# Moving the adaLN steps and the norm's scale and bias in a two-layer decoder trunk

## The chip, the cores and the metric

One core of a Trainium2 chip runs the whole program. The metric is device time in microseconds (us). A core has five engines that run side by side, each through its own instructions in order: TensorE (PE, matrix multiplication), VectorE (DVE), ScalarE (ACT), GpSimd (POOL) and SyncE (SP), which here issues all the DMAs that load data.

## What is computed

A trunk of two layers on 512 tokens of width 1024, all in float32. Each layer has three sub-layers: a SwiGLU feed-forward part (FFN), a token mixer (retention, dilated attention and stick-breaking attention on one input projection) and a second FFN. Each is modulated by a shift, a scale and a gate which come from the vector `c` (adaLN), and each ends in a norm:

```python
cond = jax.nn.silu(c)
for l in range(DEPTH):                                   # DEPTH = 2
    mod = cond @ w_ada[l] + b_ada[l]                     # (1024) x (1024, 9 * 1024)
    sh1, sc1, g1, sh2, sc2, g2, sh3, sc3, g3 = split(mod, 9)
    y = swiglu(x * (1 + sc1) + sh1, ffn1_w_gate[l], ffn1_w_up[l], ffn1_w_down[l])
    x = post_norm(x, y, g1, 0.5, ln_gain[l, 0], ln_bias[l, 0])
    y = token_mixer(x * (1 + sc2) + sh2, w_in[l], w_out[l])
    x = post_norm(x, y, g2, 1.0, ln_gain[l, 1], ln_bias[l, 1])
    y = swiglu(x * (1 + sc3) + sh3, ffn2_w_gate[l], ffn2_w_up[l], ffn2_w_down[l])
    x = post_norm(x, y, g3, 0.5, ln_gain[l, 2], ln_bias[l, 2])
# post_norm(x, y, gate, w, gain, bias) = layer_norm(ALPHA * x + w * (1 + gate) * y) * gain + bias
```

## The kernel before

**Tiles.** The residual `xall` is kept in the core as four tiles of 128 tokens by 1024 (`xres[t]`). The input of a sub-layer, `hT`, is its modulated transpose (128 by 8 by 512). All matrix products are made in three passes from a rounded high part and the remainder: `unit` (lines 168 to 178) loads 512 KB of weights into a buffer `raw`, ACT rounds it to `hi` (line 176) and VectorE subtracts to get `lo` (line 177). `raw` has three buffers, `hi` and `lo` four each. `mm3` (181 to 183) and `rows_mm` (375, 376, 379) are the three passes on TensorE.

**An FFN** (`ffn`) has 11 groups of gate and up columns, each of four units, every unit 24 matmuls; `glu` (391 to 394) makes the activation of a group. The first group's units are loaded ahead, by the sub-layer before, and its tokens are run in two halves of 256: the second half of `hT` is not there yet. Then 18 units of the down projection run over all tokens, and the last four (`RES`) token tile by token tile, with the norm of each tile behind it. The first FFN of layer 0 has three columns done in the startup.

**The norm** (`PostNorm`). `tile(t)` adds the product to the residual (312, 313), takes the statistics (315, 318), the inverse root on POOL (145, 146), the shift `nmr` (330), and normalises on ACT (331), without gain and bias: these are folded into the scale and shift columns of the next input. `head` makes the first half of the next input from tiles 0 and 1, and `rest`, called in the next sub-layer after three units of its first group, makes the second half, both through `make_h`: transposes on TensorE (275), scale and shift on ACT (279) and VectorE (281), rounding on ACT (285), remainder on VectorE (286). Each passes through `htmp`, which has three buffers. `rest` then puts gain and bias into the residual itself by eight POOL instructions of 128 by 1024 (lines 365 and 366, two for each tile), issued behind the last inverse root.

**The adaLN steps** (`ada`). A vector of 1024 values of `mod` takes eight steps (each loads 512 KB of `w_ada` into a `raw` buffer and adds it, times a column of `cond`, to an accumulator on VectorE, lines 198 to 202), a sum over partitions on POOL (206) and a small end on VectorE (215, 216 or 219). The steps stand in a list `bg`: 63 entries in the first FFN, 53, 43 and 13 in the three others; the mixers have none. `drain(3)` issues three of them after each group and `drain(2)` two after each down unit. On VectorE a step is ordered behind `mods["nmr"]`, the `nmr` of the last norm tile. Accumulators, sums, gates, and the rows of gain and bias share four buffers (`bcp`).

**Order.** The program's order is a priority; a scheduler lays out each engine's queue from it at compile time, and each queue then runs in order. `issue_after` is a constraint on that layout. So a DMA on SP that waits for a buffer holds the DMAs behind it.

**A mixer** works through ten projection jobs of two units each (`sk`, `dv`, `dq`, `dk`, `rv`, `rv2`, `rq`, `rk`, `rg`, `rg2`), whose matmuls fill TensorE between the steps of the three kinds of heads. `drain(1)` at the end of a job finds an empty list.

Of the kernel before, what the change touches and what calls it, by code (L numbers as in the profile page):

```python
# [13 lines left out]
ALU = mybir.AluOpType  # L14
# [4 lines left out]
T = 512  # L19
NT = T // P  # L20
KC = D // P
FF = 2816
NF = FF // P
# [44 lines left out]
def trunk(ctx: ExitStack, tc: tile.TileContext, x_in, c_in, w_ada, b_ada, ln_gain, ln_bias,  # L68
          f1g, f1u, f1d, w_in, w_out, f2g, f2u, f2d, rope_t, decay_t, logc_t, out, depth=DEPTH):
    nc = tc.nc  # L70
    V, S, G, PE = nc.vector, nc.scalar, nc.gpsimd, nc.tensor
# [78 lines left out]
    xres = [xall[:, t, :] for t in range(NT)]  # L150

    def gain_col(l, s):
        o = (l * 3 + s) * KC
        return cols[:, o:o + KC]
# [9 lines left out]
    mods = {}  # L164
# [79 lines left out]

    POST = 3
    bg = []

    def drain(n):
        for _ in range(min(n, len(bg))):
            bg.pop(0)()  # L250


    def new_h():
# [40 lines left out]

    class PostNorm:
        def __init__(self, l, s, nxt):
            self.l, self.s, self.nxt = l, s, nxt
            self.gate = mods[("g", l, s)]
            self.gain = bcast_row(ln_gain[l, s])
            self.bias = bcast_row(ln_bias[l, s])  # L300
            self.h = None
            if nxt is not None:
                self.h = new_h()
                self.a, self.b = ab(nxt[0], nxt[1], gain_col(l, s), bias_col(l, s))
# [55 lines left out]
        def rest(self):  # L360

            ends = make_h(1, self.h, self.a, self.b)
            with tc.issue_after(self.last.ins):
                for t in range(NT):
                    G.tensor_tensor(out=xres[t], in0=xres[t], in1=self.gain, op=ALU.mult)
                    G.tensor_tensor(out=xres[t], in0=xres[t], in1=self.bias, op=ALU.add)
            return ends


# [37 lines left out]
    REST_AT = 3  # L407
    REST_AT_Q = 3
    LAST_CUT = (256, 256, 512, 1024)
    DRAIN = (3, 2)  # L410
    RES = 4
    ACT_HEADS = (1, 3)
    OUT_EARLY = 2
# [5 lines left out]
    def ffn(l, s, wg, wu, wd, h, pre, gt, rest, prefetch, nxt):  # L419
        hh, hl = h  # L420
        ends = None
        groups = []
        f = len(gt)
        while f < NF:
            n = 2 if f + 2 <= NF else 1
            groups.append((f, n))
            f += n
        for gi, (f, n) in enumerate(groups):
            pss = [[psum() for _ in range(n)] for _ in range(2)]
            first = gi == 0 and pre is not None  # L430
            if gi == 1 and ends:
                with tc.issue_after(ends[0].ins), tc.issue_after(ends[1].ins):
                    us = gu_units(l, wg, wu, f, n)
            else:
                us = pre if first else gu_units(l, wg, wu, f, n)
            for sl in ((slice(0, 256), slice(256, 512)) if first else (slice(0, 512),)):
                for ui, (wi, k0, kn, (uh, ul)) in enumerate(us):
                    if first and sl.start == 0 and ui == REST_AT:
                        ends = rest()
                    for kk in range(kn):  # L440
                        k = k0 + kk
                        for m in range(n):
                            ms = slice(m * P, (m + 1) * P)
                            mm3(pss[wi][m][:, sl], uh[:, kk, ms], ul[:, kk, ms], hh[:, k, sl], hl[:, k, sl],
                                k == 0, k == KC - 1)
            for m in range(n):
                gt.append(glu(pss[0][m], pss[1][m]))
            drain(DRAIN[0])
        pss = [[psum() for _ in range(2)] for _ in range(NT)]

        def stat(k, t):
            ts = slice(t * P, (t + 1) * P)
            return gt[k][:, 0, ts], gt[k][:, 1, ts]
        for i in range(NF - RES):
            w = unit(wd[l, i * P:(i + 1) * P, :])
            for t in range(NT):
                rows_mm(pss[t], stat(i, t), w, t, i == 0, False)
            drain(DRAIN[1])
        drain(1000)
        ws = [unit(wd[l, i * P:(i + 1) * P, :]) for i in range(NF - RES, NF)]  # L460
        npre = prefetch()
        pn = PostNorm(l, s, nxt)
        for t in range(NT):
            rows_tail(pss[t], [(stat(i, t), ws[i - (NF - RES)]) for i in range(NF - RES, NF)])
            if t == 2:
                pn.head()
            pn.tile(t, pss[t])
        return pn, npre
# [35 lines left out]
    def mixer(l, h, pre, rest, prefetch, nxt):  # L504
# [35 lines left out]
        def job_T(name, evac):  # L540
            us = weights(name)
            pss = [psum(), psum()]
            yield from mm_T(pss, us, slice(0, 512))
            evac(pss)
            drain(1)

        def job_tok(name, evac):
            us = weights(name)
            ps = [psum(), psum()]
            for b in range(2):  # L550
                yield from mm_tok(ps, us, (2 * b, 2 * b + 1))
                evac(b, ps[b].rearrange("p (t c) -> p t c", t=2))
            drain(1)

        jobs = []

# [338 lines left out]
        for pair in range(2):  # L895
# [3 lines left out]
            for n, _ in enumerate(mm_T(ps_q, pre[2:4], slice(pair * 256, pair * 256 + 256))):  # L899
                if pair == 0 and n == REST_AT_Q:  # L900
                    ends = rest()
# [225 lines left out]
```

## Time and profile before

| | us |
|---|---|
| median of 3 runs | 2020.14 |
| lowest and highest run | 2016.13, 2021.21 |
| the profiled execution, its own time | 2018.21 |
| its span in the trace | 2016.5 |

The mean granted TensorE clock of the profiled execution is 0.99 of full speed. The program in time: startup to about 55 us, first FFN to 387, mixer to 628, second FFN to 1008, and layer 1 with an FFN to 1384, a mixer to 1626 and an FFN to the end. An entry is the place where a sub-layer's input is made from the norm of the one before. In the rows below "idle before" is the time that an engine stood still ahead of an instruction, and the arrow tells what ended it; TensorE's records overlap, so a matmul that is recorded with 0.39 us is followed by the next after some 0.23 us.

### The profile page before, as it was taken

The numbers are of one execution on the slowest core, as the hardware profiler recorded it, in microseconds if no ns is written. First come the engines' busy times: TensorE is split into PE (matmuls) and PEld (weight loads), VectorE is DVE, ScalarE is ACT, GpSimd is POOL, SyncE is SP. The second block draws the span as 40 slices with busy tenths as digits, with TensorE's granted clock in tenths as the row PEclk, the third lists the DMA queues.
The fourth block names the chain that finished last, engine by engine and source line by source line (L and its number), as shares of the span: only waits on it lengthen the run. The fifth ranks groups of instructions, "written<-read, shape, count | busy, mean of one in ns | idle before, by whom it ended". The sixth has DMA issues, their size and how long they took to land.

```text
span 2016.5 us, 24796 instructions
## 1 busy us (share of the span) xinstructions
PE 1956.5 (97%) x9984; PEld 1642.8 (81%) x9984; DVE 1149.9 (57%) x1465; ACT 689.3 (34%) x955; POOL 377.1 (19%) x236
## 2 busy tenths in 40 slices
PE   7999999999998999999989999999999989999997
PEld 5888887888887888878878888888888878888886
DVE  7655566666668746464494555327566696333325
ACT  3332212347643323321232222224566432222211
POOL 5011123142212301111041102103222041000002
PEclk9999999999999999999999999999999999999999
DMA  9555466332213455455335454422322225332231
GB/s 291 182 165 159 153 205 227 125 103 79 69 58 98 151 158 165 148 188 169 103 123 159 156 157 158 156 94 73 116 81 70 84 73 179 99 100 94 94 100 57
DMA packets 177931, 263.13 MB, mean 130 GB/s; under 512 B 8602, under 2 KB 144274, under 8 KB 177816
## 3 DMA queue, kind: packets, MB, share of 16 engines
q1 hardware_dynamic: 177816, 261.55, 40.9%
q8 instruction: 78, 1.28, 0.2%
q14 instruction: 37, 0.30, 0.0%
HBM read 259.42 MB, written 2.10 MB: 130 GB/s over the span
## 4 chain that ended last, share of the span: by engine, by line
PE 64%; issue 17%; DVE 8%; DMA 6%; ACT 2%; POOL 1%; SPq 1%; DVEq 0%; POOLq 0%; ACTq 0%
PE ps L181 16%; PE ps L182 15%; PE ps L183 15%; PE ps L376 4%; PE ps L379 4%; PE ps L375 4%; DMA raw<-in_w_ada_dram 3%; DVE acc L202 2%; DVE lo L177 1%; PE ps L599 1%; DMA raw<-in_ffn_w_down_dram 1%; DVE st L315 1%; DVE xall L313 1%; PE ps L275 1%; DMA raw<-in_ffn_w_up_dram 1%
## 5 line engine op out<-in xcount | busy, mean ns | idle before, releaser
L177 DVE TENSOR_TENSOR lo<-raw,hi 128x1024 fp32r<-128x1024 f32 (+1 forms) x302 | 441.1, 1466 | 445.8 <-ACT hi L176 445.6
L176 ACT CAST hi<-raw 128x1024 fp32r<-128x1024 f32 (+1 forms) x302 | 315.1, 1046 | 779.7 <-PE ps L182 374.5
L181 PE MATMUL ps<-hT_hi,hi 128*128 128x512 f32 x1472 | 574.2, 392 | 3.0 <-ACT hT_hi L1042 3.0
L182 PE MATMUL ps<-hT_lo,hi 128*128 128x512 f32 x1472 | 574.2, 390 | 0.3 <-DVE hT_lo L1043 0.2
L183 PE MATMUL ps<-hT_hi,lo 128*128 128x512 f32 x1472 | 573.9, 390 | 0.0
L181 PEld LDWEIGHTS ps<-hT_hi,hi 128*128 128x128 f32 x1472 | 276.3, 188 | 63.8 <-ACT hT_hi L1042 4.2
L183 PEld LDWEIGHTS ps<-hT_hi,lo 128*128 128x128 f32 x1472 | 276.7, 188 | 57.9
L182 PEld LDWEIGHTS ps<-hT_lo,hi 128*128 128x128 f32 x1472 | 276.9, 188 | 57.5 <-DVE hT_lo L1043 1.3
L202 DVE SCALAR_TENSOR_TENSOR acc<-raw,cond,acc 128x1024 f32<-128x1024 f32 x118 | 172.3, 1461 | 171.4 <-DMA raw<-in_w_ada_dram 166.3
L376 PE MATMUL ps<-lo,gT 128*128 128x512 f32 x576 | 225.1, 391 | 4.1 <-DVE lo L177 4.0
L375 PE MATMUL ps<-hi,gT 128*128 128x512 f32 x576 | 225.0, 391 | 3.0 <-DVE sg L392 3.0
L206 POOL PARTITION_ALL_REDUCE red<-acc x16 | 100.4, 6274 | 619.6 <-DVE acc L202 619.6
L379 PE MATMUL ps<-hi,gT 128*128 128x512 f32 x576 | 178.1, 391 | 0.0
L146 POOL TENSOR_TENSOR rstd<-rstd,mhalf 128x1 f32<-128x1 f32 x24 | 15.5, 645 | 624.1 <-DVE rstd L145 621.4
L376 PEld LDWEIGHTS ps<-lo,gT 128*128 128x128 f32 x576 | 108.5, 188 | 28.3 <-DVE lo L177 5.8
L375 PEld LDWEIGHTS ps<-hi,gT 128*128 128x128 f32 x576 | 108.6, 188 | 26.4 <-DVE sg L392 3.8
L379 PEld LDWEIGHTS ps<-hi,gT 128*128 128x128 f32 x576 | 108.5, 188 | 22.7
L391 ACT ACTIVATE sg<-ps 128x512 f32<-128x512 f32 x88 | 51.7, 592 | 160.2 <-PE ps L183 160.2
L181 PE MATMUL ps<-hi,hT_hi 128*128 128x256 f32 x320 | 93.7, 293 | 0.0
L182 PE MATMUL ps<-lo,hT_hi 128*128 128x256 f32 x320 | 90.4, 283 | 0.0
L183 PE MATMUL ps<-hi,hT_lo 128*128 128x256 f32 x320 | 90.3, 282 | 0.0
L392 DVE TENSOR_TENSOR sg<-sg,ps 128x512 f32<-128x512 f32 x88 | 57.4, 682 | 28.6 <-PE ps L183 28.6
(400 smaller groups left out, 2533.8 us busy)
## 6 DMA issues: line engine op xcount, KB each, us to landing
raw<-in_w_ada_dram SPq DMA_DIRECT2D x128, 512.0 KB, 3.4
raw<-in_ffn_w_down_dram SPq DMA_DIRECT2D x88, 512.0 KB, 3.5
raw<-in_ffn_w_gate_dram SPq DMA_DIRECT2D x85, 512.0 KB, 3.7
raw<-in_ffn_w_up_dram SPq DMA_DIRECT2D x85, 512.0 KB, 3.6
raw<-in_w_in_dram SPq DMA_DIRECT2D x48, 512.0 KB, 3.8
ada<-in_w_ada_dram SPq DMA_DIRECT2D x32, 256.0 KB, 5.2
raw<-in_w_out_dram SPq DMA_DIRECT2D x16, 512.0 KB, 3.5
bcrow<-in_ln_gain_dram SPq DMA_DIRECT2D x6, 512.0 KB, 5.5
```

The lines of the kernel that those rows point to most:

```text
L176: S.copy(out=hi, in_=raw)
L177: mods["dve"] = V.tensor_tensor(out=lo, in0=raw, in1=hi.bitcast(F32), op=ALU.subtract)
L181: PE.matmul(dst, lhsT=sh, rhs=mh, start=first, stop=False)
L182: PE.matmul(dst, lhsT=sh, rhs=ml, start=False, stop=False)
L183: return PE.matmul(dst, lhsT=sl, rhs=mh, start=False, stop=last)
L202: mods["dve"] = V.scalar_tensor_tensor(out=acc, in0=raw, scalar=cond[:, k:k + 1], in1=acc, op0=ALU.mult, op1=ALU.add)
L206: G.partition_all_reduce(st["red"], st["acc"], P, bass_isa.ReduceOp.add)
L375: PE.matmul(ps2[hf], lhsT=sh, rhs=wh[:, cs], start=first, stop=False)
L376: PE.matmul(ps2[hf], lhsT=sh, rhs=wl[:, cs], start=False, stop=False)
L379: PE.matmul(ps2[hf], lhsT=sl, rhs=wh[:, cs], start=False, stop=last)
L391: S.activation(out=sg, in_=ps_g, func=AF.Silu)
L392: V.tensor_tensor(out=sg, in0=sg, in1=ps_u, op=ALU.mult)
```

## The change

Three things change. The adaLN steps are ordered on VectorE behind the last split of `rest` (`ends[1]`, the last line 286 of the second half of the next input) and no longer behind the last `nmr`. They are issued by a pacer, one share after each weight unit (of a first group only in its second half), so that the list ends three units ahead of the last four; `drain(1000)` behind it stays. And gain and bias are put into the residual by eight VectorE instructions in place of the eight on POOL, one after each unit from the second group on (so over groups two and three of an FFN), in a mixer one after each of the first eight jobs; each is ordered behind the last weight split or adaLN step issued.

```diff
+    affine = []
+    def settle(n):
+        for _ in range(min(n, len(affine))):
+            with tc.issue_after(mods["dve"].ins):
+                mods["dve"] = affine.pop(0)()
+
+    def pacer(units):
+        rate, owed = len(bg) / units, 0.0
+        while True:
+            owed += rate
+            n = int(owed)
+            owed -= n
+            drain(n)
+            yield
...
     class PostNorm:
         def __init__(self, l, s, nxt):
+            assert not affine
...
             ends = make_h(1, self.h, self.a, self.b)
-            with tc.issue_after(self.last.ins):
-                for t in range(NT):
-                    G.tensor_tensor(out=xres[t], in0=xres[t], in1=self.gain, op=ALU.mult)
-                    G.tensor_tensor(out=xres[t], in0=xres[t], in1=self.bias, op=ALU.add)
+            mods["nmr"] = mods["dve"] = ends[1]
+            for t in range(NT):
+                affine.append(lambda t=t: V.tensor_tensor(out=xres[t], in0=xres[t], in1=self.gain, op=ALU.mult))
+                affine.append(lambda t=t: V.tensor_tensor(out=xres[t], in0=xres[t], in1=self.bias, op=ALU.add))
             return ends
...
-    DRAIN = (3, 2)
+    AHEAD = 3
...
+        pace = pacer(4 * sum(n for _, n in groups) // 2 + NF - RES - AHEAD)
...
+                    if sl.stop == T:
+                        next(pace)
+                        if gi > 0:
+                            settle(1)
             for m in range(n):
                 gt.append(glu(pss[0][m], pss[1][m]))
-            drain(DRAIN[0])
...
-            drain(DRAIN[1])
+            next(pace)
         drain(1000)
...
             evac(pss)                      # job_T and job_tok of the mixer
-            drain(1)
+            settle(1)
```

## Rows read from the trace of the kernel before

**Rows 1.** The page, busy time of the engines, share of the span, instructions.

```profile
PE 1956.5 (97%) x9984; PEld 1642.8 (81%) x9984; DVE 1149.9 (57%) x1465; ACT 689.3 (34%) x955; POOL 377.1 (19%) x236
```

**Rows 2.** Waits of TensorE, whole span: who waited for whom: total us, times, longest.

```profile
PE ps L275 <- ACT htmp L279: 23.8, 5, 6.5
PE ps L376 <- DVE lo L177: 4.0, 2, 2.0
...
PE ps L375 <- DVE sg L392: 3.0, 1, 3.0
```

**Rows 3.** Timeline of TensorE, second FFN's entry: start, us, line, [idle before].

```profile
644.70 1.47 PE L275 MATMUL ps<-ident,xall 128*128 128x128 f32 x10
...
655.64 0.69 PE L275 MATMUL ps<-ident,xall 128*128 128x128 f32 x2 [6.51 <-ACT htmp L279]
```

**Rows 4.** Timeline of VectorE, second FFN's entry.

```profile
640.61 2.34 DVE L330 SCALAR_TENSOR_TENSOR nmr<-mv,rstd 128x1 f32<-128x1 f32 x1 [0.72 <-POOL rstd L146]
642.88 10.10 DVE L202 SCALAR_TENSOR_TENSOR acc<-raw,cond,acc 128x1024 f32<-128x1024 f32 x3
652.89 1.44 DVE L281 TENSOR_SCALAR htmp<-ps,a_col,b_col 128x256 f32<-128x256 f32 x3
```

**Rows 5.** Timeline of POOL, second FFN's entry.

```profile
640.54 4.74 POOL L365 TENSOR_TENSOR xall<-xall,bcrow 128x1024 f32<-128x1024 f32 x2
```

**Rows 6.** Groups of instructions by line, whole span: count, busy us, mean ns.

```profile
L177 DVE TENSOR_TENSOR lo__5091<-raw,hi__5090 128x1024 fp32r<-128x1024 f32 x1 | 1.2, 1228 | 0.3 <-ACT hi__5090 L176 0.3
...
L365 POOL TENSOR_TENSOR xall<-xall,bcrow 128x1024 f32<-128x1024 f32 x20 | 49.7, 2505 | 16.3 <-PE ps L275 16.3
...
L176 ACT CAST hi<-raw 128x1024 fp32r<-128x1024 f32 (+1 forms) x302 | 315.1, 1046 | 779.7 <-PE ps L182 374.5
```

**Rows 7.** Stretches: from:to, length, PE busy (matmuls), granted clock, DMA share, GB/s.

```profile
655.60:660.20 4.60, 4.56 (x22) 0.50 0.10 33
660.20:667.00 6.80, 6.80 (x58) 0.99 0.28 84
1035.20:1039.10 3.90, 3.81 (x18) 0.50 0.10 33
...
1654.00:1656.90 2.90, 2.89 (x14) 0.50 0.09 30
...
410.00:414.50 4.50, 4.50 (x25) 0.62 0.00 0
...
895.10:899.20 4.10, 4.05 (x11) 0.58 0.74 226
```

**Rows 8.** Timelines of TensorE and VectorE, head ahead of layer 1's first FFN.

```profile
1008.34 0.88 PE L275 MATMUL ps<-ident,xall 128*128 128x128 f32 x6 [0.80 <-ACT xall L331]
...
1012.65 0.44 PE L275 MATMUL ps<-ident,xall 128*128 128x128 f32 x2
...
1014.85 0.68 DVE L286 TENSOR_TENSOR hT_lo<-htmp,hT_hi 128x512 fp32r<-128x512 f32 x1
```

**Rows 9.** Timeline of SP, second FFN's entry; then the page's median time to landing.

```profile
646.39 3.71 SPq L175 DMA_DIRECT2D raw<-in_ffn_w_gate_dram  x2
...
raw<-in_ffn_w_gate_dram SPq DMA_DIRECT2D x85, 512.0 KB, 3.7
```

**Rows 10.** Waits of SP's queue, whole span: total us, times, longest.

```profile
SPq L292 <- POOL xall L365: 35.5, 2, 17.7
```

**Rows 11.** A stretch of TensorE around 323.93, columns as in rows 7.

```profile
322.00:330.00 8.00, 6.07 (x27) 1.00 0.69 250
```

**Rows 12.** Timeline of VectorE at the end of the second FFN's gate and up.

```profile
891.43 3.06 DVE L200 TENSOR_SCALAR acc<-raw,cond 128x1024 f32<-128x1024 f32 x1 [1.56 <-DMA raw<-in_w_ada_dram]
894.42 0.67 DVE L392 TENSOR_TENSOR sg<-sg,ps 128x512 f32<-128x512 f32 x1
```

**Rows 13.** Stretches, all engines: PE, PEld, DVE, ACT, POOL busy, clock, DMA share, GB/s.

```profile
411.00:628.00 217.00, 216.81 (x1443) 186.43 (x1442) 139.55 (x251) 119.89 (x198) 52.42 (x57) 0.99 0.26 84
660.00:890.00 230.00, 230.00 (x1054) 192.13 (x1054) 130.74 (x122) 67.05 (x85) 32.88 (x9) 1.00 0.51 161
```

More of the change, by code (lines that the diff above doesn't have):

```diff
@@ L552, in job_tok @@
                 evac(b, ps[b].rearrange("p (t c) -> p t c", t=2))
-            drain(1)
+            settle(1)
         jobs = []
```

## The prediction

> **What bounds the kernel now.** I read the busy times first: TensorE is busy in 97% of the span, VectorE in 57% [rows 1]. So time can only be won where TensorE stands still or runs slowly; an engine that is merely relieved wins nothing. Next the waits of TensorE alone [rows 2]. They are short, and the largest by far is that of the transposes of `make_h` (line 275) for ACT's `htmp`: 23.8 us in 5 waits, one for each of the five entries. Three of them, at the FFN entries, are 6.5 us each (one stands in [rows 3], the twins at 1035 and 1654); the two mixer entries share the remaining 23.8 - 19.5 = 4.3. Behind them stand 4.0 us for `lo` in two waits in the first FFN's down projection and 3.0 us for `sg` where the second FFN turns from gate and up to down.
>
> Then why the FFN entries wait. On VectorE the last `nmr` takes 2.34 us for a column of 128 numbers, then three adaLN steps take 10.10 us together, and only then the first scale and shift of `make_h` (line 281) starts, at 652.89 [rows 4]. The last pair of transposes waits for `htmp` to come free, which passes through those VectorE instructions; TensorE stops until 655.64. Beside `nmr` and the steps POOL runs gain and bias, from 640.54 on [rows 5]. The same kind of two-input VectorE instruction takes 1.228 us alone [rows 6] and 10.10 / 3 = 3.37 us here.
>
> Last the clock. Behind each of these stops the granted clock is 0.50 for some microseconds, the lower level, 1.2 GHz: 22 matmuls take 4.60 us, where 58 take 6.80 right after, at 0.99 [rows 7]. A stall thus costs more than its wait.
>
> **The change part by part.** *The adaLN steps move behind the last split of `rest`.* At the FFN entries `nmr` is followed by `make_h` at once. How fast that is without them I take from a head, where the same code runs with no steps in it: from its first transposes at 1008.34 to the last pair at 1012.65 are 4.31 us [rows 8]. At the entry the transposes start at 644.70 [rows 3], so the last pair could start at 649.0; it started at 655.64 after 6.51 us idle, so TensorE ran dry at 649.1. The wait closes, 3 x 6.5 = 19.5 us. With it goes the slow clock: 22 + 18 + 14 = 54 matmuls in 4.6 + 3.9 + 2.9 = 11.4 us, against 54 x 6.80 / 58 = 6.3, so 5.1 us [rows 7]. Together 24.6.
>
> What is late next there: the weights of group two. Their loads need `raw` buffers, and the steps' loads stand ahead of them in SP's queue. Today the first gate load goes out at 646.39, at the end of the first step, and lands about 3.7 us later [rows 9]. In the head the last split ends 2.9 us after the last pair of transposes [rows 8], so here at 651.9; the first step behind it ends 1.2 us later at 653.1, the load that it lets go lands at 656.8, and ACT (1.05) and VectorE (1.23) have it ready at 659.1 [rows 6]. TensorE needs it after the second half of group one, 96 matmuls x 6.80 / 58 = 11.3 us after 649.0, at 660.3. That is a margin of 1.2 us at the second FFN, where three steps stand ahead; two do in layer 1's first FFN (43 entries over 59 units), none in the last (13). I take 0.3 us left at each entry and 1.2 for that thin margin: 2.1 off, 22.5 won. By bounds: all 24.6, or 12.6 if rival B costs its 12.
>
> *POOL's eight instructions go.* POOL itself, with 2.5 us for each [rows 6], is no bound. At the two mixer entries no steps stand in the way, and the 4.3 us come from splits slowed beside POOL. They go, with their slow clock: 25 matmuls in 4.50 us against 2.9, 1.6 us each, the twin at 1407 alike [rows 7]. 4.3 + 3.2 = 7.5; I take 7.0, since the head's 4.31 us leaves the last pair close to the point at which TensorE runs dry here too. SP also loses a stop: it stood 17.7 us at each mixer entry, because the load of the next norm's row waits for the gain buffer that POOL frees [rows 10]. No TensorE wait hangs on it [rows 2], so I count nothing for it.
>
> *The pacer.* Lumps of three and two become 63 / 53 = 1.2, 53 / 59 = 0.9, 0.7 and 0.2 steps for each unit. The two `lo` waits in the first FFN's down part stand where two steps and a weight unit share three `raw` buffers, at 250 GB/s around the first wait [rows 11]; with 1.2 the buffers turn over 2.2 times in a unit instead of 3. I take 3 of the 4.0 us. The 3.0 us for `sg` come from a step that first waited for its DMA (1.56) and then ran 3.06 us ahead of the activation [rows 12]; the clock behind it costs 1.5: 11 matmuls of 512 columns in 4.1 us, against 11 x 2 x 6.80 / 58 = 2.6, the 58 being of 256 [rows 7]. A pacer can set a step there again, so half of 4.5, 2.3. Together 5.3, between 0 and 8.5; each step that newly meets a group's end could cost as much as that one did, so -4.5 is the bound below.
>
> *Gain and bias on VectorE.* Forty instructions at 1.228 us [rows 6]: 49 us of VectorE. The 24 in the FFNs I count at nothing: eight in the 45 us of groups two and three (8 x 24 matmuls at 2 x 6.80 / 58) add 9.8 us, which raises VectorE from 131 / 230 = 57% of the time to about 79% [rows 7, 13], and weights are split up to four units ahead. Without that cover they would cost 24 x 1.2 = 29 us. The 16 in the mixers lie in chains: stick-breaking and dilated heads hand each block from TensorE to ACT and VectorE and back. VectorE is idle there in 217 - 140 = 77 us [rows 13], but an instruction may start just ahead of one that the chain needs. The trace has none of this kind; the bounds are 0 and 16 x 1.228 = 19.7 us, and I take a quarter, 5, since TensorE has job matmuls to fill with. Behind such an instruction stand the head's next VectorE step, its ACT step and TensorE's next product.
>
> The buffers of gain and bias are now held until the seventh and eighth of these instructions, in a mixer over seven jobs. The next norm's rows wait for them in SP's queue, with job weights behind. The scheduler must set that load behind the weights whose split the instruction follows; then it waits little. Bounds 0 and the 17.7 us of today's stop, of which one job ahead (48 matmuls, some 11 us) hides more than half; I take nothing.
>
> **The sum.** 22.5 + 7.0 + 5.3 = 34.8 won, 5 lost: 29.8. The profiled execution's own time is 2018.2 us, so 1988.4. The median of the runs is 1.9 above it, inside their spread of 5; I predict 1988.
>
> A rule on the clock bears on what is left over. Above, the trace shows 0.50 behind the 6.5 us stops and 0.62 over the stretch behind a mixer's 2 us stop [rows 7], but 1.00 around the `lo` wait of 2.0 us in the first FFN [rows 11]. The Trainium skill ("TensorE: Matmul & The Clock Gate", section "HAM oscillation — how this bites in real kernels") tells that an idle stretch on TensorE throttles its clock and that the burst behind it starts cold. If each of the five remainders still paid for a cold start as the mixers do now, 5 x 1.6 = 8 us would stay, and the sum would be 1996; the rows show both outcomes for stops of 2 us, and my remainders are shorter.
>
> **The rivals.** *A, the mixers pay in full.* Every VectorE instruction there delays TensorE by its length: 1988.4 + 14.7 = 2003. For it: TensorE is fed by chains in the mixers; against it: 77 us of idle VectorE and no TensorE wait in a mixer among the sizeable ones [rows 2]. *B, the wait moves to the weights of group two.* The steps hold the three `raw` buffers until after the last split; if the margin of 1.2 us fails by a whole load and split, about 6 us, and 2 of clock, the second FFN gives 8 back and layer 1's first FFN 4: 2000. *C, slower.* In the mixers POOL's small products run beside the new instructions; if each took the 3.37 us of contention and all of it reached TensorE, 16 x 3.37 = 54 us against 34.8 won give 2037. It decides from 34.8 / 16 = 2.2 us reaching TensorE for each. Against it: POOL's long instructions, beside which 3.37 was measured, are gone. *D, no change.* The layout of the queues is made anew; the steps could still be laid ahead of what TensorE needs, or the last `nmr` and ACT could be late by themselves, with the entries as slow as now: 2018. The head [rows 8] speaks against it.
>
> **How the numbers follow.** Forecast 0.66, A 0.13, B 0.08, C 0.06, D 0.07. The first three are faster by over 0.3% (6 us, about what a measurement of this kernel can tell from no change), 0.87; D within it, 0.07; C slower, 0.06. The range goes down to 1978, all of 24.6 + 7.5 + 8.5 = 40.6 won with no loss in the mixers, and up to 2006: A's 2003 with the 3 us that a margin of the pacer might cost on top. It leaves out C and D, 0.13.
>
> **What would show it.** In the new trace TensorE's wait for `htmp` falls from 23.8 us to under 3, the granted clock stays near 1.00 through 640 to 660, `nmr` takes 0.2 us, and no instruction 202 stands between it and line 281. POOL has no line 365 or 366; VectorE has 40 new ones near 1.23 us. The `lo` and `sg` waits are mostly gone. Wrong would be: a wait for `hi` or `lo` at the start of group two (B), new TensorE waits or slow stretches between 411 and 628 (A, C), or line 281 as late as now (D).

## The result and the profile after

The changed kernel takes 1993.74 us (median; 1992.21 to 1994.47), the kernel before 2018.14 in the four runs of this comparison (2015.86 to 2021.21): a ratio of 0.988 with a 95% interval of [0.986, 0.990]. Forecast were 1988 and a range of 1978 to 2006. The profiled execution took 1994.01 us with a span of 1992.3, the mean granted clock 0.996 instead of 0.99.

First the page's busy line, answering [rows 1], and then TensorE's waits, answering [rows 2] (who waited for whom: us in total, times, longest). The diff moves the lines: 292 is the old 275, 298 the old 281, 303 the old 286, 348 the old 330, 393 and 394 the old 375 and 376, 410 the old 392; 383 and 384 are gain and bias on VectorE.

```profile
PE 1950.4 (98%) x9984; PEld 1636.2 (82%) x9984; DVE 1126.7 (57%) x1505; ACT 689.7 (35%) x955; POOL 276.4 (14%) x196
```

```profile
PE ps L393 <- DVE sg L410: 7.4, 2, 4.9
...
PE ps L394 <- DVE lo L177: 1.8, 2, 1.3
PE ps L770 <- DVE d_sc L758: 1.5, 4, 0.4
...
PE ps L722 <- ACT sb_hi L711: 0.9, 2, 0.4
PE ps L723 <- DVE sb_lo L712: 0.7, 2, 0.3
```

The 23.8 us for `htmp` are gone to the last tenth. The wait for `sg`, at the turn from gate and up to down, has grown from 3.0 to 7.4 us and is now the largest. Waits of the mixers' heads (lines 722, 723, 770) are new. VectorE got 40 instructions more and is busy 23 us less.

The second FFN's entry, TensorE and then VectorE (start, us, line; idle before), answers [rows 3, 4]; the third fence has stretches of the changed kernel (columns as in rows 13), at this entry and behind the two stops for `sg`.

```profile
645.55 1.47 PE L292 MATMUL ps<-ident,xall 128*128 128x128 f32 x10
...
649.91 0.44 PE L292 MATMUL ps<-ident,xall 128*128 128x128 f32 x2
```

```profile
641.45 0.16 DVE L348 SCALAR_TENSOR_TENSOR nmr<-mv,rstd 128x1 f32<-128x1 f32 x1 [0.72 <-POOL rstd L146]
647.14 1.47 DVE L298 TENSOR_SCALAR htmp<-ps,a_col,b_col 128x256 f32<-128x256 f32 x3 [5.53 <-PE ps L292]
648.52 1.89 DVE L303 TENSOR_TENSOR hT_lo<-htmp,hT_hi 128x512 fp32r<-128x512 f32 x3
...
652.30 3.92 DVE L202 SCALAR_TENSOR_TENSOR acc<-raw,cond,acc 128x1024 f32<-128x1024 f32 x3
658.24 1.23 DVE L177 TENSOR_TENSOR lo<-raw,hi 128x1024 fp32r<-128x1024 f32 x1 [2.01 <-ACT hi L176]
```

```profile
645.00:665.00 20.00, 20.00 (x155) 19.14 (x155) 13.35 (x17) 9.69 (x15) 0.00 (x0) 1.00 0.43 132
...
275.00:279.00 4.00, 4.00 (x13) 3.11 (x12) 0.00 (x0) 1.51 (x2) 4.00 (x1) 0.57 0.18 69
...
889.50:893.50 4.00, 4.00 (x11) 3.12 (x12) 3.96 (x6) 1.46 (x2) 0.00 (x0) 0.57 0.77 235
```

From the first transposes to the last pair are 4.36 us, as in the head (4.31), without idle time and at clock 1.00. The three steps take 3.92 us where they took 10.10.

**Where the time went.** Both programs have the same 9984 matmuls, so the start of each in one trace can be set against the same one in the other. (The head's transposes ahead of layer 1, for instance, start at 1008.34 in [rows 8] and now at 1002.65: 5.7 us won by then.) The growth of that difference over a stretch is what the stretch won (minus) or lost. The stretches of an FFN run from the end of its gate and up, over the down projection, to the head behind it. The table has it for the kernel after and for the experiments below, against the trace of before, in us.

| | three FFN entries | two mixer entries | two mixers | first FFN, gate/up's end and down | second FFN, the same | layer 1's first FFN, the same | rest | total |
|---|---|---|---|---|---|---|---|---|
| after | -25.7 | -7.3 | +4.5 | +1.8 | +1.9 | 0.0 | +0.7 | -24.2 |
| e1_order | -9.7 | +0.2 | 0.0 | +3.4 | -0.5 | 0.0 | +0.3 | -6.2 |
| e2_order_affine | -25.2 | -8.7 | +4.5 | +2.9 | +0.4 | 0.0 | +0.9 | -25.4 |
| e3_affine | -25.0 | -6.9 | +4.5 | +1.4 | -1.9 | 0.0 | +1.0 | -27.0 |
| e4_pacer | -9.6 | 0.0 | 0.0 | +5.4 | +1.9 | +0.1 | +0.4 | -1.8 |
| e5_guard | -25.3 | -8.7 | +4.7 | -0.6 | -3.0 | 0.0 | +1.1 | -31.8 |
| e6_mixer_none | -25.5 | -8.1 | -0.1 | +3.9 | +0.6 | 0.0 | +0.1 | -29.2 |
| e7_best | -25.7 | -8.7 | +2.1 | -1.6 | -2.8 | 0.0 | -0.5 | -37.1 |
| e8_lumps_guard | -25.7 | -8.5 | +4.5 | +22.1 | +11.1 | +9.0 | +0.6 | +13.1 |
| e11_lumps_skip | -25.2 | -9.3 | +4.4 | +8.6 | -4.9 | 0.0 | -0.1 | -26.6 |
| e9_shift | -25.6 | -9.0 | +2.3 | -4.7 | -4.9 | 0.0 | +1.0 | -40.9 |
| e12_pause | -25.7 | -7.1 | +4.5 | -2.8 | -4.9 | 0.0 | +0.7 | -35.4 |

Entries and mixers come out alike in every kernel that treats them alike; the turns to the down projection do not. That is where the forecast went wrong.

### The profile page after: what moved, and what is told of

It reads as the page before. It is cut to its first block, busy times and chain, and to the rows that moved or that the text cites. A ratio compares the mean times of both kernels' runs of the same rounds, so it can differ in the third digit from the quotient of the medians.

```text
span 1992.3 us, 24796 instructions
## 1 busy us (share of the span) xinstructions
PE 1950.4 (98%) x9984; PEld 1636.2 (82%) x9984; DVE 1126.7 (57%) x1505; ACT 689.7 (35%) x955; POOL 276.4 (14%) x196
## 4 chain that ended last, share of the span: by engine, by line
PE 71%; DVE 10%; DMA 9%; ACT 5%; issue 3%; POOL 1%; SPq 1%; DVEq 0%; ACTq 0%; POOLq 0%
PE ps L181 16%; PE ps L183 16%; PE ps L182 16%; PE ps L394 6%; PE ps L393 6%; PE ps L397 6%; DMA raw<-in_w_ada_dram 6%; DVE lo L177 2%; ACT rtmp L650 1%; DVE acc L202 1%; DMA raw<-in_ffn_w_gate_dram 1%; ACT hi L176 1%; PE ps L292 1%; DMA raw<-in_ffn_w_up_dram 1%; DVE sg L410 1%
## 5 line engine op out<-in xcount | busy, mean ns | idle before, releaser
L177 DVE TENSOR_TENSOR lo<-raw,hi 128x1024 fp32r<-128x1024 f32 (+1 forms) x302 | 404.4, 1343 | 402.7 <-ACT hi L176 402.1
L202 DVE SCALAR_TENSOR_TENSOR acc<-raw,cond,acc 128x1024 f32<-128x1024 f32 x118 | 156.6, 1327 | 215.7 <-DMA raw<-in_w_ada_dram 215.3
L206 POOL PARTITION_ALL_REDUCE red<-acc x16 | 107.9, 6745 | 827.4 <-DVE acc L202 827.4
L394 PEld LDWEIGHTS ps<-lo,gT 128*128 128x128 f32 x576 | 108.8, 189 | 25.2 <-DVE lo L177 2.6
L411 ACT CAST gT<-sg 128x512 fp32r<-128x512 f32 x88 | 53.0, 620 | 93.7 <-DVE sg L410 93.4
```

Source lines behind the costliest of these rows:

```text
L177: mods["dve"] = V.tensor_tensor(out=lo, in0=raw, in1=hi.bitcast(F32), op=ALU.subtract)
L202: mods["dve"] = V.scalar_tensor_tensor(out=acc, in0=raw, scalar=cond[:, k:k + 1], in1=acc, op0=ALU.mult, op1=ALU.add)
L206: G.partition_all_reduce(st["red"], st["acc"], P, bass_isa.ReduceOp.add)
L394: PE.matmul(ps2[hf], lhsT=sh, rhs=wl[:, cs], start=False, stop=False)
L411: S.copy(out=g[:, 0, :], in_=sg)
```

## The experiments

Medians, range, and the ratio to the kernel before with its 95% interval:

| | us | lowest, highest | ratio |
|---|---|---|---|
| e1_order | 2010.01 | 2004.14, 2011.95 | 0.995 [0.993, 0.997] |
| e2_order_affine | 1990.85 | 1990.33, 1992.79 | 0.986 [0.984, 0.988] |
| e3_affine | 1991.33 | 1989.97, 1993.91 | 0.986 [0.984, 0.988] |
| e4_pacer | 2015.82 | 2013.88, 2018.43 | 0.999 [0.998, 1.000] |
| e5_guard | 1984.85 | 1983.93, 1986.44 | 0.983 [0.982, 0.985] |
| e6_mixer_none | 1989.97 | 1989.04, 1990.65 | 0.986 [0.984, 0.988] |
| e7_best | 1983.49 | 1981.07, 1984.84 | 0.983 [0.981, 0.985] |
| e8_lumps_guard | 2029.76 | 2028.15, 2031.88 | 1.006 [1.004, 1.008] |
| e9_shift | 1979.36 | 1977.30, 1982.69 | 0.981 [0.979, 0.982] |
| e10_shift4 | 1981.38 | 1978.83, 1982.26 | 0.981 [0.980, 0.983] |
| e11_lumps_skip | 1992.37 | 1991.56, 1995.29 | 0.988 [0.986, 0.989] |
| e12_pause | 1981.78 | 1978.92, 1984.80 | 0.982 [0.979, 0.984] |

### The change taken apart: e1 to e4

**e1_order** is the kernel before with the order alone: in `rest`, ahead of POOL's eight instructions,

```diff
             ends = make_h(1, self.h, self.a, self.b)
+            mods["nmr"] = ends[1]
```

> The kernel before with one change: the adaLN steps are ordered behind the last split of the next input. Gain and bias stay on POOL, the lumps of three and two stay. Theory (the FFN entries are slow for two reasons, the three steps and POOL beside them): the FFN entries become like the mixer entries of before, where no steps stand in the way but POOL does: a TensorE wait of some 2.2 us and 1.6 us of slow clock in place of 6.5 and 1.7. That is 4.4 us for each of three, so 13 us faster than before: 2005 us. The steps and the splits of group two then run beside POOL at 3.4 us each, which may cost up to 5 us at the second FFN. Rival (the order alone is what the change won): all of the FFN entries' 25 us, 1993 us.

It took 2010.0: 9.7 us won at the FFN entries, not 22.5. VectorE and then POOL at the second FFN's entry:

```profile
644.51 2.35 DVE L330 SCALAR_TENSOR_TENSOR nmr<-mv,rstd 128x1 f32<-128x1 f32 x1 [0.72 <-POOL rstd L146]
...
651.60 4.03 DVE L286 TENSOR_TENSOR hT_lo<-htmp,hT_hi 128x512 fp32r<-128x512 f32 x3
...
658.42 10.11 DVE L202 SCALAR_TENSOR_TENSOR acc<-raw,cond,acc 128x1024 f32<-128x1024 f32 x3
668.45 1.21 DVE L177 TENSOR_TENSOR lo<-raw,hi 128x1024 fp32r<-128x1024 f32 x1
```

```profile
644.44 4.75 POOL L366 TENSOR_TENSOR xall<-xall,bcrow 128x1024 f32<-128x1024 f32 x2
...
660.72 6.72 POOL L367 TENSOR_TENSOR xall<-xall,bcrow 128x1024 f32<-128x1024 f32 x2
```

With the steps out of the way `nmr` still takes 2.35 us, three splits 4.03 instead of 1.89, and the steps behind them 10.11 as before. The first `lo` of group two is ready at 669.7, ten us later than after the whole change, and TensorE waits for it. Its waits in this kernel, whole span:

```profile
PE ps L275 <- ACT htmp L279: 10.6, 5, 2.2
...
PE ps L183 <- DVE lo L177: 3.9, 3, 1.8
```

The five waits for `htmp` that are left are 2.2 us at most, as the theory had it. The waits for `lo` (line 183) are rival B's mechanism: one wait for the weights of group two at each FFN entry, 3.9 us together. It exists, but in these runs only where POOL runs beside.

**e2_order_affine** is the changed kernel with the lumps in the pacer's place, `drain(3)` after each group and `drain(2)` after each down unit.

> The changed kernel with the lumps of three and two in place of the pacer. Theory (the pacer cost 3 to 4 us, by steps laid ahead of the last activation of gate and up in the first and second FFN): 3.5 us faster than the changed kernel, 1990 us, with the waits for lo of the first FFN's down part back (4 us) and the wait for sg small. Rival (the pacer won the 5.3 us of the prediction, and the loss is elsewhere): 5 us slower than the changed kernel, 1999 us.

1990.85, with the entries and mixers of the changed kernel. TensorE's waits for `lo` in the down projections are back (4.5 us), as the theory had it, but that for `sg` isn't small (4.1 us), and in layer 0's two FFNs this kernel loses 3.3 us on the kernel before, the changed one 3.7. So between pacer and lumps lie 0.4 us in these stretches, 1.2 in the whole traces and 2.9 in the medians, whose ranges just overlap: the pacer's net is nothing, or a loss of up to 3 us, and not the gain that was forecast.

**e3_affine** takes the order away as well, so that gain and bias on VectorE are all that is left of the change:

```diff
-            mods["nmr"] = mods["dve"] = ends[1]
+            mods["dve"] = ends[1]
```

> Gain and bias on VectorE, but the adaLN steps ordered behind the last nmr as before, and lumps of three and two in place of the pacer. At the FFN entries three steps still stand ahead of the scale and shift of the next input. Theory (the three steps cost the entry because they ran beside POOL): nmr ends at once and three steps take 3.9 us in place of 10.1, so the scale and shift can start about when the first transposes are done; the TensorE wait at the FFN entries is under 0.7 us, and the time is that of the run with order and VectorE together, 1990 us. Rival (any step ahead of the split costs its length): 3.9 us of wait and 1.6 of clock at two or three FFN entries stay, some 14 us, 2004 us.

1991.33, the same. VectorE at the second FFN's entry:

```profile
642.19 0.16 DVE L348 SCALAR_TENSOR_TENSOR nmr<-mv,rstd 128x1 f32<-128x1 f32 x1 [0.72 <-POOL rstd L146]
642.27 3.92 DVE L202 SCALAR_TENSOR_TENSOR acc<-raw,cond,acc 128x1024 f32<-128x1024 f32 x3
647.86 1.46 DVE L298 TENSOR_SCALAR htmp<-ps,a_col,b_col 128x256 f32<-128x256 f32 x3 [1.68 <-PE ps L292]
```

The steps stand where they stood before the change, right behind `nmr`, and VectorE then still idles 1.68 us until TensorE's transposes arrive. Relieved of POOL they fit into a gap. Of the entries' 25.7 us the relief of POOL is worth 25.0 by itself, the order 9.7 by itself, and the order behind the relief 0.7 at most.

**e4_pacer** is the kernel before with the pacer alone.

> The kernel before with the pacer alone: steps behind the last nmr, gain and bias on POOL. The pacer sets three steps in the first group of the second FFN, two in layer 1's first, none in its last. Theory: the second FFN's entry stays at 6.5 us of wait, layer 1's first loses one step of 3.4 us, its last falls to the 2.2 us of an entry with POOL alone: 3.4 + 4.5 won; the pacer's own 3.5 us lost inside the FFNs: 4 to 5 us faster than before, 2014 us. Rival (the pacer wins 5.3 us inside the FFNs): 13 us faster, 2005 us.

2015.82. It wins 9.6 us at the entries, chiefly at the last (-6.6), where few steps are left to stand in the way, and gives 7.3 back in the two FFNs of layer 0. The waits show the trade:

```profile
PE ps L286 <- ACT htmp L290: 17.0, 5, 6.6
PE ps L386 <- DVE sg L403: 8.2, 3, 3.9
```

`htmp` falls from 23.8 to 17.0, `sg` rises from 3.0 to 8.2.

### The turn to the down projection: e5, e8, e11, e12

In the changed kernel two stops make the 7.4 us, one in each FFN of layer 0. TensorE's lines come first, then VectorE and SP at the second turn:

```profile
274.53 0.50 PE L393 MATMUL ps<-hi,gT 128*128 128x512 f32 x1 [2.44 <-DVE sg L410]
...
889.32 0.61 PE L393 MATMUL ps<-hi,gT 128*128 128x512 f32 x1 [4.94 <-DVE sg L410]
```

```profile
882.45 0.68 DVE L410 TENSOR_TENSOR sg<-sg,ps 128x512 f32<-128x512 f32 x1
887.39 1.28 DVE L202 SCALAR_TENSOR_TENSOR acc<-raw,cond,acc 128x1024 f32<-128x1024 f32 x1 [4.26 <-DMA raw<-in_w_ada_dram]
888.59 0.68 DVE L410 TENSOR_TENSOR sg<-sg,ps 128x512 f32<-128x512 f32 x1
```

```profile
882.55 0.33 SPq L198 DMA_DIRECT2D raw<-in_w_ada_dram  x1
```

Between the two halves of the last activation stands a step whose load went out only at 882.55 and landed at 887.4. VectorE idles 4.26 us in front of it, and TensorE, which has nothing but this activation to go on with, stops for 4.94. The first turn, VectorE again, is milder and a little different:

```profile
266.66 1.28 DVE L202 SCALAR_TENSOR_TENSOR acc<-raw,cond,acc 128x1024 f32<-128x1024 f32 x1 [2.38 <-DMA raw<-in_w_ada_dram]
...
271.45 1.29 DVE L202 SCALAR_TENSOR_TENSOR acc<-raw,cond,acc 128x1024 f32<-128x1024 f32 x1
272.65 1.22 DVE L177 TENSOR_TENSOR lo<-raw,hi 128x1024 fp32r<-128x1024 f32 x1
273.79 0.68 DVE L410 TENSOR_TENSOR sg<-sg,ps 128x512 f32<-128x512 f32 x1
```

A step waits 2.38 us for its load ahead of the activation, and from then on VectorE works without a break; a second step, which waits for nothing, and a split stand in that row before the last `sg`. Behind each of the two stops the granted clock is 0.57 over four microseconds (above), most of it at the lower level, 1.2 GHz.

POOL has a part in such stops. In the kernel before, the step of [rows 12] that ran 3.06 us ahead of `sg` is of a kind that takes 0.74 us elsewhere (line 200, a step with no accumulator to read yet); beside it ran POOL's sum over partitions:

```profile
889.41 6.34 POOL L206 PARTITION_ALL_REDUCE red<-acc  x1 [32.25 <-DVE acc L202]
```

So by an estimate from these two durations 2.3 of the 3.0 us of that stop go with the step's neighbour, and not with its place alone.

**e5_guard** lets no step out after the last two units of gate and up; those two steps follow the activation and are ordered behind it on VectorE:

```diff
-                        next(pace)
+                        if gi < len(groups) - 1 or ui < len(us) - HELD:      # HELD = 2
+                            next(pace)
...
+            if gi == len(groups) - 1:
+                mods["nmr"] = mods["glu"]          # last instruction of the activation
+                for _ in range(min(HELD, len(us))):
+                    next(pace)
```

> The changed kernel, but the pacer issues no step after the last two units of the last gate and up group; those two steps follow the group's activation and are ordered behind it on VectorE. Theory (the pacer lost time because a step whose load had not landed stood ahead of the activation): the two stops for sg with the slow clock behind them, 2.6 + 1.5 and 4.9 + 1.5 = 10.5 us, go, and 1993.7 becomes about 1983; TensorE's sg wait falls from 7.4 us to under 1. Rival (steps held back only delay the weights of the down projection): the sg wait becomes a lo wait of like size, and the time stays at 1991 or more.

1984.85, 8.9 less than the changed kernel. No `sg` wait is left; in its place stand 2.7 us for `hi` in the first FFN and 1.7 for `lo` in the second. So both theories had a part: most of the stop goes, and some turns into a wait for down weights.

**e8_lumps_guard** does the same to the lumps: in e2_order_affine the last group's three steps are ordered behind the activation.

```diff
+            if gi == len(groups) - 1:
+                mods["nmr"] = mods["glu"]
             drain(3)
```

> Steps in lumps of three for each group and two for each down unit as before the change, with the order and gain and bias of the change; the last group's three steps are ordered behind its activation. Theory (lumps or pacer matter only through the steps ahead of the activation): the sg wait, 4.1 us in the run with lumps, goes, and its 1991 becomes about 1986; the lo waits of 4.5 us in the first down projection stay. Rival (a spread over units is better in itself): 3 us or more behind the paced kernel with held steps even where lo waits are left out.

A plain miss: 2029.8 instead of 1986, 39 us above e2_order_affine and slower than before. VectorE and SP at the first turn:

```profile
267.11 0.69 DVE L410 TENSOR_TENSOR sg<-sg,ps 128x512 f32<-128x512 f32 x1 [8.83 <-PE ps L183]
...
269.09 1.28 DVE L202 SCALAR_TENSOR_TENSOR acc<-raw,cond,acc 128x1024 f32<-128x1024 f32 x1
270.29 0.74 DVE L200 TENSOR_SCALAR acc<-raw,cond 128x1024 f32<-128x1024 f32 x1
271.07 6.76 DVE L202 SCALAR_TENSOR_TENSOR acc<-raw,cond,acc 128x1024 f32<-128x1024 f32 x2
277.74 1.22 DVE L177 TENSOR_TENSOR lo<-raw,hi 128x1024 fp32r<-128x1024 f32 x1
```

```profile
253.34 17.38 SPq L198 DMA_DIRECT2D raw<-in_w_ada_dram  x2
271.06 0.33 SPq L175 DMA_DIRECT2D raw<-in_ffn_w_down_dram  x1
...
277.85 0.33 SPq L175 DMA_DIRECT2D raw<-in_ffn_w_down_dram  x1
...
290.34 0.33 SPq L175 DMA_DIRECT2D raw<-in_ffn_w_down_dram  x1
```

The first steps behind the activation run without waiting for a load: they had been loaded, and held the `raw` buffers, while VectorE idled 8.83 us ahead of it. SP issues one step's load at 253.34, the next only when a buffer comes free at the first of these steps, and down weights behind it: one load of them had left before, at 247.43, the next leave at 271.06 and 277.85, then one at 290.34. POOL adds to it here: of the two steps from 271.07 one takes 5.44 us, beside a sum over partitions from 270.51 to 277.02. TensorE stops for `hi` and `lo` throughout the down projections:

```profile
PE ps L394 <- DVE lo L177: 21.1, 11, 3.4
PE ps L393 <- ACT hi L176: 13.7, 3, 5.0
```

So a step behind the activation is no better than one ahead of it, if its load has taken the buffer that a down unit needs. That this, and not the lumps of two behind it or POOL, makes most of the 39 us is argued from these rows; the next run takes the last group's lump away.

**e11_lumps_skip** therefore issues no lump for the last group at all (the list is then emptied by the lumps of two):

```diff
-            drain(3)
+            if gi < len(groups) - 1:
+                drain(3)
```

> Lumps of three and two with the order and gain and bias of the change; the last group of gate and up issues no lump at all. Theory (the 39 us lost when that lump stood behind the activation came from its loads ahead of the down weights): no such loss; the sg wait of 4.1 us of the run with lumps goes, 1991 becomes about 1986. Rival (the loss came from ordering the steps behind the activation, or the lumps of two in the down projection alone are too much for the loads): sg or lo stops of 4 us or more stay, 1991 or more.

1992.37: the 39 us are not lost, and at the second turn the whole 4.9 us came back, as the theory had it, but in the first FFN 8.6 were lost, where the rival had it. So the sum is the lumps' 1991 again. The 63 entries of that list are too many for what is left: 27 go with nine groups, and 36 by twos take all 18 units. Some 2.4 us are lost over these units, 2.6 where the last four then wait for their weights, and 3.6 at the head behind them.

**e12_pause** is the changed kernel with the pacer pausing over those two units, nothing caught up, its rate a little higher elsewhere:

```diff
-        pace = pacer(4 * sum(n for _, n in groups) // 2 + NF - RES - AHEAD)
+        pace = pacer(4 * sum(n for _, n in groups) // 2 + NF - RES - AHEAD - HELD)
...
-                        next(pace)
+                        if gi < len(groups) - 1 or ui < len(us) - HELD:
+                            next(pace)
...
+            if gi == len(groups) - 1:
+                mods["nmr"] = mods["glu"]
```

> The changed kernel with one difference: the pacer pauses over the last two units of the last gate and up group, its rate a little higher elsewhere; gain and bias stay where the change put them. Theory (the pacer itself is a gain, and all of its loss lies at the turn to the down projection): the stops there go, 7.4 us for sg and about 3 of slow clock, and 1993.7 becomes 1982 to 1983; against the lumps of three and two (1990.9) the paused pacer is then worth 8 us, more than the 5.3 that the prediction took for the pacer. Rival (the best kernel so far owes its time to the moved places in the mixers): 1986 or more.

1981.78, 12.0 us less than the changed kernel, by the pause and the order that goes with it. Its waits at the turns are 0.6 us for `sg` and 1.1 for `lo`, and the stretch around the first turn (columns as in rows 13) runs at the full clock:

```profile
PE ps L394 <- DVE lo L177: 1.1, 1, 1.1
...
PE ps L393 <- DVE sg L410: 0.6, 1, 0.6
```

```profile
268.00:280.00 12.00, 11.36 (x50) 8.99 (x49) 7.52 (x7) 2.17 (x3) 0.00 (x0) 1.00 0.50 164
```

From the turn on, the two FFNs of layer 0 win 7.8 us on the kernel before, where the changed kernel loses 3.7 and the lumps of e11_lumps_skip, which also leave the turn free, lose 3.6. The spread is a gain, once no step stands at the turn.

### The mixers: e6, e7, and what is best: e9, e10

**e6_mixer_none** leaves gain and bias of the mixers' eight `settle` calls out: `affine.pop(0)` without the call.

> The changed kernel without the 16 gain and bias instructions of the two mixers: the residual of these two sub-layers is left without gain and bias. Theory (the instructions delay chains of the heads, seen in the trace as +2.2 us in each mixer): 4.5 us less, about 1989. Rival (the mixers' loss lies in another place, such as the rows of gain and bias held longer in SP's queue, or in noise): within 1.5 us of the changed kernel, 1992 to 1994.

1989.97, 3.8 less than the changed kernel, and in the table the mixers go from +4.5 to -0.1: their whole loss hangs on these 16 instructions. In the changed kernel's first mixer VectorE, then POOL, shows how:

```profile
533.88 2.30 DVE L384 TENSOR_TENSOR xall<-xall,bcrow 128x1024 f32<-128x1024 f32 x1
536.10 0.15 DVE L756 RECIPROCAL d_den<-d_den 128x2 f32<-128x2 f32 x1
536.29 1.44 DVE L758 TENSOR_SCALAR d_sc<-d_sc,d_den 128x384 f32<-128x384 f32 x2
```

```profile
532.95 2.14 POOL L653 TENSOR_TENSOR rq<-rq,rtmp 128x512 f32<-128x512 f32 x1
```

A bias of 2.30 us stands right ahead of the scaling of a dilated head (`d_sc`), for which TensorE then waits. It is slowed by its neighbour: of the changed kernel's forty new instructions 34 take 1.21 to 1.22 us, and six, all in the mixers and each beside an instruction of POOL, 1.48 or 2.30. That is rival C's contention, at a smaller price.

**e7_best** moves two of the eight, on top of e5_guard: three after the job `sk`, none after `rv` and `rk`, the two jobs whose instruction stood just ahead of a head's step.

> The kernel with the two held steps, and in the mixers two of the eight gain and bias instructions moved: none after the jobs rv and rk, three after sk instead of one. Theory (each of the moved instructions stood just ahead of a step that a head's chain needed): 2 to 3 us less than the kernel with the held steps alone, about 1980.5. Rival (any place costs the same, since the instruction meets another chain): the same time as the kernel with the held steps.

1983.49, 1.4 less than e5_guard by the medians, whose ranges touch; in the traces the mixers' loss fell from 4.7 to 2.1. The place matters, by about half of the loss.

**e9_shift** joins the places of e7_best with the pause of e12_pause.

> The kernel with the moved gain and bias places, but the two steps held back are not caught up behind the last group's activation: the pacer pauses over the last two units and its rate is a little higher elsewhere. Theory (a load of a step that stands ahead of the first down weights costs the remaining stop for hi and lo at the turn to the down projection, 2.5 + 1.8 us and some slow clock): these stops go, and 1983.5 becomes about 1980. Rival (that stop comes from POOL's reduction beside VectorE, which took one step 5.44 us there, not from the held steps): the stop stays, 1983.

1979.36, the best: 38 us under the kernel before, 14 under the changed one. No stop is left at the turns beyond 0.3 us for `lo`, so the rival, which had it stay, falls as a forecast. As a cause it isn't excluded: in e5_guard a step took 5.44 us beside POOL's reduction at this turn (last section), and here none of the steps is slowed there.

**e10_shift4** widens the pause to four units (`HELD = 4`).

> As the kernel with the paused pacer, but the pause covers four units, the whole last group of gate and up. Theory of the steps' loads: no worse than with two units, 1979 to 1981. Theory of a supply limit: the down projections carry more steps for each unit and wait for lo there, 1983 or more.

1981.38, level with e9_shift within the spread of the runs; 3.7 us lost in the first FFN's gate and up, and new waits of gate and up units for `hi` (1.0 us) and `lo` (0.8) in the whole span. The down projections don't wait for `lo`, so the supply limit of the second theory isn't met there.

## Why the prediction was right and wrong

**Right: what bounds the kernel, and the size of the entries.** TensorE's waits named the places. The FFN entries gave 25.7 us, 22.5 forecast and 24.6 the upper bound, which was 1.1 too low; the mixer entries 7.3, 7.0 forecast. No remainder is left: the `htmp` wait is 0, the clock 1.00 over the entry. The rule of the Trainium skill by which remainders of stops would go on paying a cold start, and which gave 1996, found no stop to act on here. At the two turns, where stops of 2.4 and 4.9 us did come, the clock behind them fell to 0.57. That a burst behind an idle stretch starts cold is what the Trainium skill tells in that section ("TensorE: Matmul & The Clock Gate", "HAM oscillation — how this bites in real kernels"); its example has waits of about 3 to 5 us, so for the stop of 2.4 us it is the trace alone that shows it.

**Right in size, wrong in cause: the order of the steps.** The 24.6 us were put down to the steps' move, and POOL's relief was credited with the mixer entries alone. The runs turn this round: the relief by itself gives 25.0 at the FFN entries, the order by itself 9.7. The prediction had seen [rows 5] and that the steps take 3.37 us instead of 1.228, and stopped there. Had it followed on: an `nmr` at 640.61 [rows 4] that takes the 0.2 us it forecast, and three steps of 1.228 [rows 6], end at 644.5, before the transposes even start at 644.70 [rows 3]. Only the sum of the two edits was forecast, so the number didn't suffer: that it was right is luck as far as the cause goes.

**Right: the weights of group two.** The first unit was forecast ready at 659.1, on a margin of 1.2 us; its `lo` came from 658.24 to 659.47, and TensorE waited for none. Rival B was right as a mechanism under POOL's contention only (e1_order).

**Right: gain and bias on VectorE.** Nothing in the FFNs; in the mixers 4.5 us, 5 forecast, between bounds of 0 and 19.7. The quarter was a choice, not a reading, and that it came so near is luck; e6_mixer_none shows that the loss is theirs. Rivals A and D didn't come, and of C only the contention, for six instructions; the longest of the heads' waits is 0.4 us. SP's two stops of [rows 10] are gone, and nothing hung on them, as assumed.

**Wrong: the pacer, 5.3 us won in the forecast, in truth 3.7 lost where they should have come.** This term is what parts 1988 from 1993.7. Of its two halves the `lo` half was too small: the two places of [rows 11] and its twin won 5.1 us, for 3 forecast; both stops went whole. The `sg` half failed. "A pacer can set a step there again, so half of 4.5" took an even chance of a gain of 4.5 at one turn, and nothing at the other, which had no stop before. Measured: 1.9 lost at the second FFN's turn, and at the first 4.5 for the stop and the slow clock with 2.4 for `lo` behind it. 5.1 won stand against 6.9 + 1.9 lost: 3.7. The bound of -4.5 in the prediction held it; the value that was taken did not. What was overlooked: with about one step after each unit, about two steps are issued after the last two units and ahead of the activation at every turn of a long list, and their loads go out late, since they wait for a `raw` buffer like any weight. What the pacer itself costs depends on what stands beside it: alone on the kernel before 7.3 us in these two stretches (e4_pacer); in the changed kernel the lumps in its place lose 3.3 of the 3.7 too.

**The sum.** 29.8 forecast, 24.2 measured: the pacer's stretches are 9.0 short, the FFN entries 3.2 and the mixers 0.5 better, mixer entries 0.3 better, the rest 0.7 worse.

**What stays open.** How much of a turn's loss belongs to the pacer and how much to the layout that the scheduler draws anew: with lumps the first FFN lost 2.9 us and the second 0.4 (e2_order_affine), without the order 1.4 and -1.9 (e3_affine). The loss follows whichever step happens to stand there. And e12_pause both pauses and orders later steps behind the activation; the two weren't tried apart. Nor was POOL's sum over partitions held apart, which lies at the second turn in e5_guard and e7_best and not in e12_pause and e9_shift; how much of the 3 to 4 us between these pairs is owed to it no run tells.

## What to carry over

Before moving slowed work out of a critical path, look at what runs beside it: taking the neighbour away may make it short enough to stay. Background work that is spread evenly needs a pause wherever the main engine has a single thing to wait for; and it must be held back with its loads, since a late order on the engine alone leaves the buffers taken. A term whose bounds lie on both sides of nothing should not enter a sum with half of its better end, unless a row says which end is nearer.

## What the runs showed of the hardware

**POOL and VectorE take turns.** In e1_order POOL's products take 2.37 us each while VectorE is nearly idle (4.75 for two) and 3.36 (6.72 for two) beside the steps, and the steps 3.37 (10.11 for three) instead of 1.31 (3.92): both go at one pace. Even `nmr`, 128 numbers, takes 2.35 us instead of 0.16: it starts 0.07 us behind POOL's first product and ends about with it. The Trainium skill states this as a lock ("SBUF — State Buffer", sections "Who interferes with whom" and "Summary: rules for kernel authors"): an instruction of VectorE with two inputs from SBUF contends with a GpSimd instruction that reads SBUF, and the one that issues second waits until the first is through. The rows agree in the main; one full turn of each would be 2.37 + 1.31 = 3.68 us, a little more than the 3.37 measured. The cost was larger than expected: with POOL's forty long instructions gone VectorE's busy time fell by 23 us, although it took forty over.

**POOL's reduction over partitions does it too.** In e5_guard a step takes 5.44 us beside one; VectorE, then POOL:

```profile
882.81 5.44 DVE L202 SCALAR_TENSOR_TENSOR acc<-raw,cond,acc 128x1024 f32<-128x1024 f32 x1
```

```profile
882.25 6.52 POOL L206 PARTITION_ALL_REDUCE red<-acc  x1 [67.20 <-DVE acc L202]
```

The step, begun 0.56 us into the reduction, ends at 888.25, the reduction at 888.77. Sixteen of these reductions stay in the changed kernel, and beside 14 of them its trace has a VectorE instruction of 1.9 to 5.2 us, mostly a weight split that takes 1.22 alone. What moving them would win wasn't tried.
